# The last 256 hidden features in front of the Strassen units, fewer adding DMAs, sums and loads at new steps

## The chip, the cores and the metric

One core of one Trainium2 chip runs the whole kernel. The metric is the time of one launch in device microseconds; the median of several runs is compared. The engines are TensorE (PE, with its weight loads PEld), VectorE (DVE), ScalarE (ACT), GpSimd (POOL) and SyncE (SP). Each works through its own instructions in order. SP issues most plain DMAs; POOL issues the DMAs that add to their destination and some stores.

## The reference

One layer over 16 meta tokens and 512 tokens of width 1024: a gated feed-forward network, a mixer of retention and selected attention, a second feed-forward network, a norm. The change lies at the mixer's end and in the second network.

```python
D_MODEL, SEQ, D_FF, N_META = 1024, 512, 2816, 16
def rmsnorm(x, g):
    y = x * lax.rsqrt(jnp.mean(x * x, axis=-1, keepdims=True) + EPS)
    return y * g
def swiglu(u, w_gate, w_up, w_down):
    return (jax.nn.silu(u @ w_gate) * (u @ w_up)) @ w_down
h = h + 0.5 * swiglu(rmsnorm(h, ffn1_norm), ffn1_w_gate, ffn1_w_up, ffn1_w_down)
h = h + hybrid_mixer(rmsnorm(h, mix_norm), ...)        # ends with merged @ w_mix_out
h = h + 0.5 * swiglu(rmsnorm(h, ffn2_norm), ffn2_w_gate, ffn2_w_up, ffn2_w_down)
return rmsnorm(h, final_norm)[:, N_META:]
```

## The kernel before

Every float32 product is made of three matmuls in a rounded format: each operand is split into an upper part (ACT copies it, `whi`) and a lower part (the rest, `wlo`), and upper x upper, upper x lower and lower x upper are summed in PSUM. The lower part is made in one of two ways: `in_two` lets DVE subtract the upper part from the source, `in_two_by_pool` lets ACT write the negative upper part and a DMA issued by POOL add the source to it ("adding DMA"; such a step is called far, `is_far`).

The mixer's last product, `merged @ w_mix_out`, is made in eight rounds (`mixed(c)`, PSUM tile `psmo`). Each adds the residual (`hc`), writes the new tokens of 128 features (`new_x`, split into `xh` and `xl`), and takes the squares for the norm.

The second network's gate and up products over 2816 hidden features are made in two kinds of work. 2560 features are five **units** of 512 features: unit u makes gate and up together as a 2x2 block product by Strassen's way with seven products instead of eight (`PRODUCTS`), each in two steps, so 14 steps a unit and 12 matmuls of 128x512 a step. For this, weights are summed (`Unit.sums`: n 0 makes `s1`, 1 makes `s2`, 3 and 4 change `21` and `12` in place) and so are tokens (T1 to T4, made by `token_sums` and split by `split_token_sum`). The PSUM tiles are `psvX`, `psvZ`, `psvY`. The remaining **256 features** (`last_run`, PSUM tile `psl`, weights in `glast`) are four steps of 24 plain matmuls with no sums, behind unit 4.

`run_units` writes the order out by hand: `ahead(i)` says how many steps ahead a step's weights are begun (ACT's upper part), `lower()` puts the lower part in the middle of a step, and `behind(i)` stands at the end of a step: evictions from PSUM, Silu, `finish(i)` of the unit before (scaling by the norm, transposes `turn`, stores `leave` to the DRAM tile `hx`), sums for this or the next unit (`SUMS`, `FIRST_SUMS`), loads for the next (`LOADS`). `norm_column` sums the squares by small matmuls (`psn`). PE, ACT and DVE keep that order (`tc.manual_schedule`); `in_order` and `pool_order` keep a DMA's place on SP or POOL.

Weights lie in a pool of pairs (`pair_of`, 128x1024 elements a tile, most tags with one buffer); a load into a pair waits until the old content has been split and summed. Units 1 and 3 keep the first halves of `12` and `21` in `f2["extra"]`. Even steps' split weights have three buffers (`whi`, `wlo`), odd ones two (`dhi`, `dlo`).

Behind the units comes the down product (`psd`, then the Strassen products X, Y, U, W, V, Z, Q with `half_product`), fed by hidden rows read back from `hx` (`read_hidden`), weights `wd2`, block sums `wx` that were made during the mixer (`block_sums`; `late_sums` makes the last of them in its rounds), and tokens read back from `ht`. `todo` and `behind` hold work that is popped in the middle of its steps.

## Time and profile before

| what | value |
|---|---|
| time, median of 3 runs | 1498.04 us (1497.08 to 1506.18) |
| the profiled execution's own time | 1496.0 us |
| its span, first to last instruction | 1494.2 us |
| mean granted TensorE clock | 0.995 |
| PE busy | 1470.4 us, 98% |
| DVE / ACT / POOL busy | 1146.6 / 803.4 / 272.9 us |
| mixer's last product (`psmo`) | 1102.0 to 1145.5 us |
| units 0 to 4 | 1145.5 to 1356.6 us |
| last 256 features (`psl`) | 1356.6 to 1378.4 us |
| down product | 1378.4 us to the end |

The page lists the busy time of each engine, DMA queues, the chain of work that ended last, and groups of instructions with their mean duration. A line such as `L2685` is a line of the kernel; `psvX<-whi,th` names the tile written and the tiles read. Views of the same trace that were asked for beside it: busy times by stretches of the span, waits (who waited for whom: total, times, longest), instructions in order of time (start, duration, engine, line, operation; in brackets the idle time before and what ended it), and groups of instructions of one engine or tile. The profile is of one execution; matmuls overlap, so their start-to-start distance is what counts.

### The profile page before, as it was taken

The page shows a single profiled execution, that of the slowest core. Times are in us where ns is not written, and L with a number is a line of the kernel's source. Part 1 is how long each engine was busy: PE and PEld are TensorE (multiplying, and loading weights), DVE is VectorE, ACT ScalarE, POOL GpSimd, SP SyncE. Part 2 cuts the span into 40 slices and gives each one's busy share as a digit, 9 for nine tenths or more (in the row PEclk, how much of TensorE's full clock was granted, in tenths as well). Part 3 has the DMA queues.
Part 4 walks back from the last instruction along what each step waited for, and adds up shares of the span by engine and source line. Part 5 has one row for each costly group of instructions (what it writes and reads, how often), then busy time and mean ns, then how long its engine had stood idle before and what let it go on. Part 6 is the DMA issues. An engine that isn't in the chain of part 4 may idle for free.

```text
span 1494.2 us, 23045 instructions
## 1 busy us (share of the span) xinstructions
PE 1470.4 (98%) x8709; PEld 1296.9 (87%) x8709; DVE 1146.6 (77%) x1718; ACT 803.4 (54%) x1200; POOL 272.9 (18%) x397
## 2 busy tenths in 40 slices
PE   9999999999999999999999999999999899999998
PEld 8999999999988888889898888898787688788886
DVE  4999999788886768677868776877568667687778
ACT  5655555566354445553434446776436666563555
POOL 1012222001110121112110121220205134344001
PEclk9999999999999999999999999999999999999999
DMA  5358988786554444679976688666757899899874
GB/s 178 86 180 270 267 265 265 264 294 208 201 174 149 165 148 153 143 211 198 235 200 177 171 227 236 187 188 182 226 196 219 235 222 233 198 224 281 301 257 147
DMA packets 212142, 312.37 MB, mean 209 GB/s; under 512 B 13440, under 2 KB 129816, under 8 KB 211136
## 3 DMA queue, kind: packets, MB, share of 16 engines
q1 hardware_dynamic: 168832, 217.91, 44.9%
q0 software_dynamic: 40672, 88.74, 25.7%
q10 hardware_dynamic: 2528, 4.27, 0.8%
q8 instruction: 68, 1.11, 0.3%
q14 instruction: 42, 0.34, 0.1%
HBM read 220.66 MB, written 63.98 MB: 190 GB/s over the span
## 4 chain that ended last, share of the span: by engine, by line
PE 81%; DMA 7%; DVE 6%; issue 3%; ACT 3%; POOL 1%; SPq 0%; POOLq 0%; ACTq 0%; DVEq 0%
PE psqX L176 7%; PE psrg L176 6%; PE psro L176 5%; PE psvX L1373 4%; PE psqY L176 3%; PE psrk L176 3%; PE psvX L2685 3%; PE psrq L176 3%; PE psga L176 3%; PE psat L176 2%; PE psX L1048 2%; PE psak L176 2%; PE psd L3021 2%; PE psgate L176 2%; PE psvY L1373 2%
## 5 line engine op out<-in xcount | busy, mean ns | idle before, releaser
L314 DVE TENSOR_TENSOR wlo<-raw,whi 128x1024 fp32r<-128x1024 f32 (+2 forms) x181 | 200.6, 1109 | 58.5 <-ACT whi L313 57.9
L313 ACT ACTIVATE whi<-raw 128x1024 fp32r<-128x1024 f32 (+2 forms) x181 | 174.9, 967 | 127.0 <-PE psX L1048 12.2
L176 PE MATMUL psro<-vo,whi 128*128 128x512 f32 x256 | 75.3, 389 | 0.0
L176 PE MATMUL psqX<-th,whi 128*128 128x264 f32 x216 | 61.5, 285 | 1.9 <-DVE g L546 1.9
L176 PE MATMUL psqX<-tl,whi 128*128 128x264 f32 x216 | 61.2, 283 | 0.0
L176 PE MATMUL psqX<-th,wlo 128*128 128x264 f32 x216 | 61.1, 283 | 0.0
L176 PEld LDWEIGHTS psro<-vo,whi 128*128 128x128 f32 x256 | 48.1, 188 | 10.0
L320 POOL DMA_DIRECT2D wlo<-raw x21 | 28.4, 1379 | 151.7 <-ACT wlo L319 55.2
L956 POOL DMA_DIRECT2D hx<-z x72 | 50.1, 810 | 21.5 <-DVE z L2758 16.6
L314 DVE TENSOR_TENSOR wlo<-w,whi 128x1024 fp32r<-128x1024 f32 x35 | 42.6, 1221 | 13.1 <-ACT whi L313 13.1
L176 PE MATMUL psrg<-xh,whi 128*128 128x512 f32 x128 | 50.5, 394 | 0.0
L176 PE MATMUL psrg<-xl,whi 128*128 128x512 f32 x128 | 50.0, 390 | 0.0
L313 ACT ACTIVATE whi<-w 128x1024 fp32r<-128x1024 f32 x35 | 36.9, 1056 | 20.6 <-PE psvX L1373 10.9
L313 ACT ACTIVATE whi<-wsum 128x1024 fp32r<-128x1024 f32 x36 | 38.1, 1058 | 17.9 <-issue 7.3
L176 PE MATMUL psro<-vo,wlo 128*128 128x512 f32 x128 | 46.4, 390 | 0.6 <-DMA wlo<-raw 0.6
L314 DVE TENSOR_TENSOR dlo<-w,dhi 128x1024 fp32r<-128x1024 f32 x23 | 28.0, 1219 | 22.8 <-ACT dhi L313 22.8
L314 DVE TENSOR_TENSOR wlo<-wsum,whi 128x1024 fp32r<-128x1024 f32 x36 | 43.5, 1220 | 0.1
L176 PEld LDWEIGHTS psqX<-th,whi 128*128 128x128 f32 x216 | 40.6, 188 | 2.5 <-DVE g L546 2.3
L176 PE MATMUL psat<-vo,whi 128*128 128x512 f32 x128 | 40.8, 400 | 1.1 <-ACT whi L117 1.1
L176 PEld LDWEIGHTS psqX<-th,wlo 128*128 128x128 f32 x216 | 40.6, 188 | 0.0
L176 PEld LDWEIGHTS psqX<-tl,whi 128*128 128x128 f32 x216 | 40.6, 188 | 0.0
L2311 POOL DMA_DIRECT2D pt<-turned x32 | 20.8, 658 | 104.6 <-DVE turned L2305 98.1
(658 smaller groups left out, 5084.6 us busy)
## 6 DMA issues: line engine op xcount, KB each, us to landing
raw<-in_w_in_dram SPq DMA_DIRECT2D x35, 512.0 KB, 5.1
raw<-in_ffn_w_down_dram SPq DMA_DIRECT2D x34, 512.0 KB, 4.5
raw<-in_w_in_dram SPq DMA_DIRECT2D x17, 1024.0 KB, 6.0
raw<-wx SPq DMA_DIRECT2D x32, 512.0 KB, 4.8
w<-in_w_in_dram SPq DMA_DIRECT2D x24, 512.0 KB, 6.4
raw<-in_ffn_w_up_dram SPq DMA_DIRECT2D x11, 1024.0 KB, 7.9
wlo<-raw POOLq DMA_DIRECT2D x21, 512.0 KB, 6.1
raw<-in_ffn_w_gate_dram SPq DMA_DIRECT2D x10, 1024.0 KB, 6.5
```

Of the source, the lines that this page charges most:

```text
L176: nc.tensor.matmul(o, a[:, k, :], b[:, sl], start=first and k == 0 and i == 0, stop=last and k == nk - 1 and i == 2, skip_group_check=onto)
L313: nc.scalar.activation(hi, src, AF.Copy)
L314: return lambda: nc.vector.tensor_tensor(lo, src, hi.bitcast(F32), ALU.subtract)
L320: return lambda: nc.gpsimd.dma_start(lo, src, accum_op=ALU.add)
L956: tc.keep_in_program_order(nc.gpsimd.dma_start(*args, **how))
L1048: nc.tensor.matmul(pss[c], a[:, k, c * P : (c + 1) * P], m[:, k, :], start=first and k == 0 and i == 0, stop=last and k == 1 and i == 2, s ...
L1373: nc.tensor.matmul(d[bank_][t], a, b[:, k, :], start=not onto and j + k + m == 0, stop=j + k == 3 and m == 2, skip_group_check=onto)
L2311: nc.gpsimd.dma_start(d.rearrange("m b k (a q) -> a k (m b) q", a=4)[a], z[32 * a : 32 * a + 32, :16].rearrange("k b j q -> k b (j q)"))
L2685: nc.tensor.matmul(d[bank_][:, t], a, b[:, k, :], start=not onto and j + k + m == 0, stop=j + k == 3 and m == 2, skip_group_check=onto)
L3021: nc.tensor.matmul(ps, a[:, bs], m[:, j, :], start=first and i == 0, stop=last and i == 2, skip_group_check=onto)
```

## The change

The 256 last features move from behind unit 4 to a place between the mixer's last product and unit 0; their weights are loaded during mixer rounds 2 to 5, and unit 0's first loads and splits move back accordingly. The token sums' splits and `norm_column` stand behind their four steps, `last_scale`, `last_turn` and `last_leave` behind unit 0's steps 0 to 2. The weights' sums leave `behind` for the middle of a step, up to a step and a half earlier. Loads for the next unit stand at most one behind a step, in another order and starting at step 0. Only steps 4, 6, 8 and 12 stay far: four adding DMAs a unit where units 1 to 4 had seven and unit 0 five; some lower parts are made one to four steps behind their upper parts. Units 1 to 4 leave out one transpose and half a store that nobody reads. The moves of the mixer's `late_sums` keep their place on POOL. At the other end, unit 4's steps 10 to 13 and the down product's first loads and splits interleave, unit 4's `finish` runs in the middle of the first four down steps, T4 gets a pool of its own (later also two hidden blocks), the down product's weights lie in a new pool, its last eviction is done in two halves, and two PSUM pools change places.

```diff
-        LOADS = {4: (("11", 0),), 5: (("21", 0),), 6: (("11", 2),), 7: (("22", 0), ("12", 0)), 8: (("21", 2),),
-                 10: (("12", 2),), 11: (("22", 2),)}
-        SUMS = {1: ((1, 2),), 2: ((3, 0),), 4: ((4, 0),), 5: ((3, 2),), 7: ((4, 2),)}
-        FIRST_SUMS = {1: ((1, 2),), 3: ((3, 0),), 5: ((4, 0), (3, 2)), 7: ((4, 2),)}
-        SPLITS = {0: ((2, 1), (4, 1)), 1: ((2, 0),), 2: ((1, 0), (1, 1)), 4: ((3, 0), (3, 1)), 7: ((4, 0),)}
+        LOADS = {0: ("12", 0), 1: ("21", 0), 2: ("11", 0), 4: ("22", 0), 5: ("11", 2), 7: ("21", 2), 9: ("12", 2), 10: ("22", 2)}
+        SUMS = {0: ((0, 2),), 1: ((1, 2), (3, 0)), 2: ((4, 0),), 4: ((4, 2),), 5: ((3, 2),)}
+        NEXT = {10: (0, 0), 11: (1, 0)}
+        UNUSED = [(u, 0, 1) for u in range(1, 5)]
...
         def is_far(self, i):
-            return i % 2 == 0 if self.u else i in (2, 3, 6, 8, 10)
+            return i in (4, 6, 8, 12)
 
         def ahead(self, i):
-            if not self.is_far(i):
-                return 3
-            return 5 if self.u else 4
+
+            first = {0: 2, 1: 2, 2: 3, 4: 4}
+            if not self.u and i in first:
+                return first[i], 0
+            return {0: (5, 4), 2: (5, 1), 10: (5, 2)}.get(i, (5 - i % 2 * 2, 0))
 
         def upper(self, i):
 
             v = self.q[self.PRODUCTS[i // 2][0], i % 2 * 2]
-            where = "raw" if not self.u and i in (2, 3) else "odd" if i % 2 and (self.u or i > 1) else None
-            return parts(v, where, (in_two, in_two_by_pool)[self.is_far(i)])
+            return parts(v, i % 2 == 1, (in_two, in_two_by_pool)[self.is_far(i)])
...
                         lower()
+                        for at in self.SUMS.get(i, ()):
+                            if self.u or at[0] > 1:
+                                self.sums(*at)
+                        if self.next and i in self.NEXT:
+                            self.next.sums(*self.NEXT[i])
...
                 p.finish(i)
-            else:
...
-                if i == 0:
-                    token_sums(KD - 1)
-                for n, at in self.SPLITS.get(i, ()):
-                    split_token_sum(n, at)
-                if i == 4:
-                    norm_column()
-                if i == 6:
-                    self.load("22", 0)
-                    self.load("22", 2)
-            for n, j in (self.SUMS if p else self.FIRST_SUMS).get(i, ()):
-                if p and n == 1:
-                    self.sums(0, j)
-                self.sums(n, j)
-            nxt = self.next
-            if nxt:
-                for n, j in self.LOADS.get(i, ()):
-                    nxt.load(n, j)
-                if i in (11, 12):
-                    nxt.sums(i - 11, 0)
-            else:
-                for g in {4: (0,), 6: (1,), 7: (2, 3)}.get(i, ()):
-                    load_last(g)
+            elif i in (0, 1, 2):
+                (last_scale, last_turn, last_leave)[i]()
+            if self.next and i in self.LOADS:
+                self.next.load(*self.LOADS[i])
...
-                nc.vector.transpose(z[:, u], self.d["H"][:, v % 2 * 2 + v // 2])
+                if (self.u, n, u) not in self.UNUSED:
+                    nc.vector.transpose(z[:, u], self.d["H"][:, v % 2 * 2 + v // 2])
...
-            z = self.d["z", n]
+            z, m = self.d["z", n], 1 + ((self.u, n, 1) not in self.UNUSED)
...
-        t = glast[g] = pair_of(("w110", "w112", "s10", "s12")[g])
+        if g not in glast:
+            glast[g] = pair_of(("w120", "w122")[g - 2])
+        t = glast[g]
         for i, w in enumerate((wg2, wu2)):
...
+            if b == 1:
                 lower()
-        for n in ((0, 3, 4, 5), (6, 7), (8, 9), (10, 12))[g]:
-            units[4].finish(n)
+        behind_last(g)
+
+    def behind_last(g):
+
+        un = units[0]
+        for n, j in {0: (("11", 2),), 1: (("12", 0), ("12", 2)), 2: (("22", 0), ("22", 2))}.get(g, ()):
+            un.load(n, j)
+        if g == 0:
+            token_sums(KD - 1)
+        elif g == 1:
+            f2["ss"] = room2(1, "ss")[:, :, : 2 * P]
+            for t in range(2):
+                nc.scalar.activation(f2["ss"][:, t].rearrange("p (b a y) -> p a b y", b=2, a=4),
+                                     ssum3[:, t * 2 * P : (t + 1) * 2 * P].rearrange("p (a b y) -> p a b y", b=2, a=4), AF.Copy)
+        elif g == 2:
+            norm_column()
+        else:
+            last_silu()
+        for n, at in {0: ((2, 1), (4, 1), (2, 0)), 1: ((4, 0), (1, 0), (1, 1), (3, 0)), 2: ((3, 1),)}.get(g, ()):
+            split_token_sum(n, at)
+        if g > 1:
+            un.sums(1, g * 2 - 4)
 
     def last_silu():
...
-                  for un in units for i in range(14)]
-        steps_ += [(lambda g=g: parts(glast[g]), lambda *a, g=g: last_run(g, *a), 2 + (g < 3)) for g in range(4)]
-        ws, begin = {}, {}
-        for i, (upper, _, ahead_) in enumerate(steps_):
-            if i > 3:
-                begin.setdefault(i - ahead_, []).append(i)
...
+        for i, (_, _, (ahead_, later_)) in enumerate(steps_):
+            begin.setdefault(i - ahead_, []).append(i)
+            end.setdefault(i - ahead_ + later_, []).append(i)
+        for j in range(2):
+            ws[j] = steps_[j][0]()
...
         for i, (_, run, _) in enumerate(steps_):
-            now = begin.get(i, ())
-            for j in now:
+            for j in begin.get(i, ()):
                 ws[j] = steps_[j][0]()
-            run(ws.pop(i)[:2], lambda: [ws[j][2]() for j in now])
+            run(ws[i][:2], lambda: [ws[j][2]() for j in end.get(i, ())])
             yield
...
         late_sums = block_sums(range(EARLY_SUMS, 8), lambda: [block_room(t) for t in ("R", "ssum2", "caus", "score3")],
-                               nc.gpsimd.dma_start)
+                               pool_order)
         cols = mo_cols
-        EARLY = {2: (("11", 0), ("11", 2)), 3: (("s1", 0),), 4: (("12", 0), ("s1", 2)), 5: (("12", 2), ("21", 0)), 6: (("21", 2),)}
+        EARLY = {2: (0,), 3: (1,), 4: (2, ("s1", 0)), 5: (3, ("s1", 2)), 6: (("21", 0),), 7: (("11", 0), ("21", 2))}
         one, two = slice(0, 2 * P), slice(2 * P, S)
         firsts, hcs = [pair_of(t) for t in ("s20", "s22")], []
-        for j in (0, 2):
-            units[0].q["11", j] = pair_of(f"w11{j}")
+        for g in range(2):
...
-                if n == "s1":
-                    units[0].added_load(j)
+            for at in EARLY.get(c, ()):
+                if at in range(4):
+                    load_last(at)
+                elif at[0] == "s1":
+                    units[0].added_load(at[1])
                 else:
-                    units[0].load(n, j, in_order)
-            if c >= 5:
+                    units[0].load(*at, in_order)
+            if c >= 6:
                 next(unit_pipe)
                 next(unit_pipe)
...
             squares_go(c)
             if c in (1, 3, 5):
                 token_sums(c)
-            if c == 6:
...
-        f2["odd"] = tts.enter_context(pool("f2d", 1, side="right"))
-        f2["z"], f2["extra"] = (wpool.tile([P, 2048], F32, tag="raw", name=name, bufs=2).rearrange("p (a k c) -> p a k c", a=2, k=2)
-                                for name in ("z", "extra"))
...
-            hid[f] = tuple(f2["hid"].tile([P, S], F32R, tag=f"h{c}{f}", name=f"h{c}") for c in "hl")
+            if f < F0:
+                hid[f] = tuple(f2["hid"].tile([P, S], F32R, tag=f"h{c}{f}", name=f"h{c}") for c in "hl")
+            else:
+                both = ttp4.tile([P, 2, S], F32R, tag=f"t{'hl'[f - F1]}4", name="hh")
+                hid[f] = both[:, 0], both[:, 1]
             return in_two(hid[f, "raw"], *hid[f])
 
...
-                        d["raw"] = wpool.tile([P, 2048], F32, tag="raw", name="raw", bufs=2).rearrange("p (k c) -> p k c", k=4)
+                        d["raw"] = fin["p"].tile([P, 2048], F32, tag="raw", name="raw", bufs=2).rearrange("p (k c) -> p k c", k=4)
...
+                        def add(bs):
+                            for b in bs:
+                                add_sums(b, slice(c * S, (c + 1) * S), d["ps"][b])
+
+                        if c:
+                            add((0, 1))
+                            behind.append(lambda add=add: add((2, 3)))
+                        else:
+                            add(range(4))
 
                 steps.append((pre, lambda at=at: d[at], run))
...
         with tc.manual_schedule(engines=BUSY):
-            for _ in range(14 * 5):
...
             f2["hid"] = hids2.enter_context(pool("hid2", 1, side="right"))
-            next(unit_pipe)
             for f in range(3):
                 read_hidden(f)
-            for i in range(3):
-                read_tokens(i)
+            next(unit_pipe)
+            units_on.close()
+            hpool = later.enter_context(pool("hpool", 1))
+            hTok.extend(hpool.tile([P, D], F32, tag=f"hTok{b}", name=f"hTok{b}") for b in range(4))
+            fp = fin["p"] = later.enter_context(pool("f2", 1))
+            homes.append(fp)
+            next(pipe)
             lows = [split_hidden(f) for f in range(2)]
             next(unit_pipe)
             for low in lows:
                 low()
             read_hidden(3)
-            lows = [split_hidden(f) for f in (2, 3)]
-            next(unit_pipe)
-            for low in lows:
-                low()
             next(pipe)
             next(pipe)
             next(unit_pipe)
             next(pipe)
-            next(pipe)
...
-            hTok.extend(hpool.tile([P, D], F32, tag=f"hTok{b}", name=f"hTok{b}") for b in range(4))
-            fp = fin["p"] = later.enter_context(pool("f2", 1))
-            homes.append(fp)
+            lows = [split_hidden(f) for f in (2, 3)]
+            for i in range(3):
+                read_tokens(i)
+            for f in (F1, F1 + 1):
+                read_hidden(f)
+            next(unit_pipe)
+            for low in lows:
+                low()
+
+            def steps_of_last(*steps):
+                for i in steps:
+                    units[4].finish(i)
 
             def begin():
 
-                last_silu()
+                steps_of_last(0, 3, 4)
                 for i in range(3):
                     take_tokens(i)
                     read_tokens(3 + i)
-                last_scale()
-                last_turn()
 
             def go_on():
 
-                last_leave()
+                steps_of_last(5, 6, 7)
                 for i in range(3, 6):
                     take_tokens(i)
                     if i < 5:
                         read_tokens(3 + i)
 
-            todo += [begin, go_on, lambda: [f(i) for f, i in ((read_hidden, F1), (read_hidden, F1 + 1), (take_tokens, 6), (take_tokens, 7))],
+            todo += [begin, go_on, lambda: (steps_of_last(8, 9, 10), take_tokens(6), take_tokens(7)), lambda: steps_of_last(12),
                      lambda: None, lambda: split_hidden(F1)(), lambda: split_hidden(F1 + 1)()]
             for _ in range(n_plain):
                 next(pipe)
             mm_done()
-            ends = later.enter_context(pool("f2px", 2, PSUM))
+            ends = later.enter_context(pool("f2pe", 6, PSUM))
+            pb["pool"] = later.enter_context(pool("f2px", 2, PSUM))
+            next(pipe)
             pb["pool"] = ends
-            next(pipe)
-            pb["pool"] = later.enter_context(pool("f2pe", 6, PSUM))
             next(pipe)
             gfb = fin["gfb"] = fp.tile([P, D], F32, tag="gfb", name="gfb")
```

More of the change, by code (lines that the diff above doesn't have):

```diff
@@ L2846, in split_token_sum @@
         part = t[:, :, 2 * P :] if n in (2, 3) else t[:, :, : 2 * P]
-        split(part, *(p[:, n - 1, 2 * i : 2 * i + 2, :] for p in f2["tt"]))
+        split(part, *(p[:, 2 * i : 2 * i + 2, :] for p in f2["tt"][n - 1]))
     def token_sums(c):
@@ L2871, in run_units @@
     def run_units():
[L2873 to L2882 removed]
+        steps_ = [(lambda g=g: parts(glast[g]), lambda *a, g=g: last_run(g, *a), (2, 0)) for g in range(4)]
+        steps_ += [(lambda un=un, i=i: un.upper(i), lambda *a, un=un, i=i: un.run(i, *a), un.ahead(i))
+                   for un in units for i in range(14)]
+        ws, begin, end = {}, {}, {}
+        for i, (_, _, (ahead_, later_)) in enumerate(steps_):
[3 more added lines that the diff above has]
+            ws[j] = steps_[j][0]()
             yield
[L2884 to L2885 removed]
+            ws[j][2]()
             yield
         for i, (_, run, _) in enumerate(steps_):
[L2888 to L2889 removed]
+            for j in begin.get(i, ()):
                 ws[j] = steps_[j][0]()
[L2891 removed]
+            run(ws[i][:2], lambda: [ws[j][2]() for j in end.get(i, ())])
             yield
@@ L2957, in mixed @@
                 token_sums(c)
-            if c == 6:
-                units[0].sums(1, 0)
         with tc.manual_schedule(engines=BUSY):
@@ L3059 @@
         todo = []
-        def keep(b, c):
-            pass
         fin = {}
@@ L3110, in leave @@
             nc.scalar.dma_start(out[rows, 512:], hTok[b][:, 512:])
-        streams, ahead, behind, homes = {}, [4], [], [wpool]
+        streams, ahead, behind, homes, spare = {}, [4], [], [wpool], ["dhi", "dlo"]
         SLOT = {0: 0, 1: 1, 2: 2, 3: 3, 4: 4, 5: 7, 6: 5, 7: 6}
@@ L3201, in sums_of @@
             return lambda j: wx[i, :, 2 * j : 2 * j + 2, :]
-        steps = down(0, 4, 4, keep)[0]
+        steps = down(0, 4, 4)[0]
         n_plain = len(steps)
         steps += product("X", rows(0, C1), 0, added((0, C1)))
-        steps += down(F1, 2, 2, keep)[0]
+        steps += down(F1, 2, 2)[0]
         steps += product("Y", sums_of(0), 4, added((1, C2)))
@@ L3216 @@
         with tc.manual_schedule(engines=BUSY):
-            for _ in range(14 * 5):
+            for _ in range(4 + 14 * 4 + 10):
                 next(unit_pipe)
```

53 lines of the change are left out of this document (19 added, 34 removed).

## The prediction

> **What bounds the kernel now.** First the page's head, for the engines' shares.
>
> ```profile
> span 1494.2 us, 23045 instructions
> PE 1470.4 (98%) x8709; PEld 1296.9 (87%) x8709; DVE 1146.6 (77%) x1718; ACT 803.4 (54%) x1200; POOL 272.9 (18%) x397
> ```
>
> PE is busy for 98% of the span. No matmul is added or taken away by the change, so all it can win are pauses of PE, and all it can lose are new ones. Next comes the view by stretches, over the part that the diff touches, cut where products begin: unit 0, units 1 to 4 (168 matmuls each), the last 256 features (96 matmuls, `psl`), the first down steps, the rest, the tail. Its columns are the stretch, its length, the busy time of PE, PEld, DVE, ACT and POOL (with instructions), PE's granted clock, the DMA engines' share and GB/s.
>
> ```profile
> 1145.50:1196.10 50.60, 43.82 (x178) 34.35 (x177) 35.17 (x39) 35.93 (x47) 13.40 (x13) 0.93 0.80 208
> 1196.10:1234.90 38.80, 38.80 (x170) 31.51 (x169) 26.29 (x27) 26.14 (x29) 11.35 (x15) 1.00 0.92 224
> 1234.90:1273.70 38.80, 38.80 (x169) 31.56 (x168) 30.31 (x33) 25.46 (x28) 15.91 (x22) 1.00 0.92 234
> 1273.70:1316.70 43.00, 39.68 (x169) 31.33 (x168) 30.31 (x34) 25.88 (x28) 16.64 (x24) 1.00 0.87 205
> 1316.70:1356.60 39.90, 39.32 (x169) 31.39 (x168) 30.78 (x33) 23.43 (x26) 15.90 (x23) 1.00 0.88 216
> 1356.60:1378.40 21.80, 21.80 (x97) 18.02 (x97) 16.09 (x22) 5.74 (x8) 10.27 (x16) 1.00 0.94 300
> 1378.40:1400.40 22.00, 22.00 (x97) 18.05 (x97) 12.67 (x20) 11.64 (x19) 2.57 (x4) 1.00 0.80 281
> 1400.40:1484.40 84.00, 84.00 (x371) 69.46 (x370) 70.95 (x97) 49.08 (x70) 4.48 (x2) 1.00 0.71 243
> ```
>
> A unit without pauses takes 38.8 us (units 1 and 2). Unit 0 takes 50.6, unit 3 43.0, unit 4 39.9: 11.8 + 4.2 + 1.1 = 17.1 us above that. From 1356.6 to 1484.4 PE never pauses, and the 9.8 us behind that are the output's, which the diff leaves as they are. The waits of PE in these stretches and the instructions that make up the first unit's norm say what the 17.1 us are:
>
> ```profile
> PE psvY L2685 <- DMA wlo<-w: 2.7, 1, 2.7
> PE psvX L2685 <- ACT th L117: 2.0, 1, 2.0
> PE psvX L2685 <- ACT part L2696: 1.8, 1, 1.8
> PE psvX L2685 <- DMA wlo<-w: 1.4, 2, 1.0
> PE psvX L2685 <- ACT dhi L313: 1.0, 1, 1.0
> PE psvY L2685 <- ACT part L2696: 0.9, 1, 0.9
> PE psvX L2685 <- DVE dlo L314: 0.5, 1, 0.5
> ```
>
> ```profile
> 1163.27 0.95 PE L2866 MATMUL psn<-ones,ss 128*128 128x1 f32 x8
> 1187.13 0.63 PE L2685 MATMUL psvY<-dlo,xh 128*128 128x512 f32 x1
> 1187.56 0.63 PE L2685 MATMUL psvY<-dhi,xh 128*128 128x512 f32 x1
> ```
>
> The pauses themselves are 10.3 us. Behind the longest ones matmuls start 0.43 us apart (the last two rows), where 38.8 / 168 = 0.231 is usual: unit 0's clock of 0.93 is that, some 3 us. 0.95 us of unit 0 are the eight `psn` matmuls, which stay. **What can be won is 17.1 - 0.95 = 16.2 us**, 1.1% of the time; 10.9 of it lie in unit 0.
>
> **The change, part by part.**
>
> *The last 256 features first.* Unit 0 pauses because its weights' sums, the token sums T1 to T4 and their splits all have to be made beside its own matmuls: `th` (a token sum) is late by 2.0, adding DMAs by 2.7 and 1.0. The last features need plain tokens and unsummed weights. Their 21.8 us (sixth stretch) now stand between the mixer and unit 0, with DVE and ACT free for those sums. Is that enough? DVE is behind when the mixer ends:
>
> ```profile
> 1149.33 0.68 DVE L2943 TENSOR_TENSOR hc<-psmo,hc 128x512 f32<-128x512 f32 x1
> ...
> 1152.38 1.75 DVE L2859 TENSOR_TENSOR s<-s,w 128x512 f32<-128x512 f32 x1
> ```
>
> ```profile
> 1230.67 1.22 DVE L2641 TENSOR_TENSOR s<-w,w 128x1024 f32<-128x1024 f32 x1
> 1231.80 1.22 DVE L314 TENSOR_TENSOR dlo<-w,dhi 128x1024 fp32r<-128x1024 f32 x1
> ```
>
> Token sums can begin at about 1152.4. A 128x1024 instruction of DVE keeps it for 1.13 us (from 1230.67 to 1231.80), one of 128x512 for 0.69. From 1152.4 DVE has three token sums (3.1 us), eight token splits (5.5), the splits of the last two groups of the last features (2.3), those of unit 0's first three steps (3.4) and two sums for `s2` (2.3): 16.6 us, done near 1169.0. Unit 0's first step starts at 1145.5 + 21.8 + 0.9 (`psn`) = 1168.2; the split it needs stands some 5 us ahead of the end of that list, and T2 is needed four steps later. I cost it at nothing. If the list ran 3 us late, the cover would still hold; at 6 us PE would wait. In the mixer's last rounds the splits of unit 0's first four steps make way for two of the last features: on DVE two for two, and one sum (1.13 us) leaves with them, so DVE is no later than now. Step 4 of unit 0 takes its operand by an adding DMA which ACT can only prepare behind `last_silu`:
>
> ```profile
> 1176.76 1.28 ACT L2738 ACT_TABLE_LOAD   x1
> L2816 ACT ACTIVATE sg<-psl,r x4: 457/470/483, 1383.2 to 1384.2; 128x256 f32<-128x256 f32 x4
> L2583 ACT ACTIVATE wlo<-w 128x1024 fp32r<-128x1024 f32 x4 | 4.2, 1043 | 0.0
> DMA to landing us min/median/max: 4.4/6.9/12.6
> ```
>
> From the end of `psl` (1168.2): table 1.3, four silus 1.6, a split 1.0, the two copies 2.0, so the DMA starts at 1174.1 and lands after 4.4 to 12.6 us, at 1181.0 by the median. Its half of step 4 begins at 1168.2 + 4 x 2.77 + 8 x 0.231 = 1181.1. PE waits between 0 and 5.6 us; I take 1.0. The Trainium skill ("DMA: Bandwidth & Descriptors", Anatomy of one DMA) fits a GpSimd transfer as 2.0 us plus bytes at 436 GB/s, an estimate of 3.2 us for 512 KB. By that fit this wait would be zero and the sum 1.0 us lower; the 4.4 us minimum here is above it, so the rows decide.
>
> *Four adding DMAs a unit instead of seven.* DMA in the five units:
>
> ```profile
> q0 software_dynamic: 7759, 25.70, 57.8%
> wlo<-w POOLq DMA_DIRECT2D x16, 512.0 KB, 9.1
> w<-in_ffn_w_up_dram SPq DMA_DIRECT2D x16, 512.0 KB, 9.2
> ```
>
> The software queue takes 57.8% of 211.5 us with 33 adding DMAs of 512 KB among its 25.70 MB (33 x 0.524 = 17.3): by bytes 82 us, an estimate of 2.5 us of all 16 engines for each. Three fewer take 7.5 of 38.8 us: the share of 0.92 falls to about 0.73, and a load lands sooner than 9.2. The price: each of the three becomes one DVE subtraction (+1.13) and saves one ACT copy (-1.0).
>
> ```profile
> L2758 DVE STREAM_TRANSPOSE z<-H 128x512 f32<-128x512 f32 x8 | 5.2, 689 | 1.9 <-DMA hx<-z 1.9
> L314 DVE TENSOR_TENSOR dlo<-w,dhi 128x1024 fp32r<-128x1024 f32 x5 | 6.1, 1217 | 4.6 <-ACT dhi L313 4.6
> ```
>
> DVE in a unit (unit 2, third stretch): 30.3 + 3 x 1.13 - 0.7 (one transpose left out) = 33.0 of 38.8, 85%. The eighth stretch ran DVE at 70.95 of 84.0, 84%, and PE never paused: so a share like this can be covered. Of unit 2's 8.5 idle us 4.6 are waits for ACT's upper part, and ACT gets 3 us lighter. Bounds for units 1 to 4 together: 0 to 4 x (33.0 + 8.5 - 38.8) = 10.8 us, if none of DVE's idle time can shrink. I take 1.0, near the row of the eighth stretch.
>
> *Sums mid step, one load a step.* Unit 3's 4.2 us:
>
> ```profile
> 1269.51 3.39 SPq L2622 DMA_DIRECT2D w<-in_ffn_w_up_dram  x2
> 1285.15 1.23 DVE L2641 TENSOR_TENSOR s<-w,w 128x1024 f32<-128x1024 f32 x1 [5.78 <-DMA w<-in_ffn_w_up_dram]
> 1288.84 0.50 PE L2685 MATMUL psvX<-dhi,th 128*128 128x512 f32 x1 [1.04 <-ACT dhi L313]
> ```
>
> The two up-loads went out from 1269.5 on and DVE stood in front of the sum of both until 1285.2, up to 15.7 us later; the matmuls of step 5 (1288.8) hang on it. The last load (`22`, second half) moves from step 11 to 10 and the one ahead of it from 8 to 7, 2.8 us each. The sum now stands in step 0 instead of behind step 1; behind it on DVE wait the previous unit's scaling, two more sums and the split of step 5, and PE waits for that split. With the loads earlier and DMA lighter I cost this at nothing beyond the 1.0 above. Pinning the `wx` moves costs nothing either: POOL is busy 16 of 39 us in a unit, and PE waits for none of them.
>
> *Handover to the down product.* Before, `psl`'s 21.8 us covered unit 4's `finish`, the reading of hidden rows and the first `wd2` loads. Now these begin at unit 4's step 9 to 13, 11 us ahead of the first down step, and `finish` runs inside down steps 0 to 3.
>
> ```profile
> raw<-in_ffn_w_down_dram SPq DMA_DIRECT2D x34, 512.0 KB, 4.5
> 1374.74 1.06 ACT L313 ACTIVATE whi<-raw 128x1024 fp32r<-128x1024 f32 x1 [1.47 <-DMA raw<-in_ffn_w_down_dram]
> ```
>
> Unit 4 loads nothing more (before, eight `glast` loads), so its queue is free. Three hidden rows and four loads of 512 KB go out between 10.9 us (end of step 9) and some 7 us (the last split, step 10) ahead of the down step; the first weights land 4.5 us later, then 1.06 on ACT and 1.13 on DVE: 10.9 - 6.7 = 4.2 us early at best, 7 - 6.7 = 0.3 at worst by the median, and with a landing of 9.2 us (the up-loads' row) 4.4 us late. I take 1.0. `finish` brings DVE its eight turns (5.2 us by the row above) and about as much again into a stretch that had 12.7 of 22.0, while the last features' scale and turn (3 us) leave it: some 20 of 21.8, tight, but its evictions have banks to spare. I keep it inside the same 4.4.
>
> **The sum**, against the profiled execution's own 1496.0 us (its span of 1494.2 and 1.8 around it): 1496.0 - 16.2 + 1.0 + 1.0 + 1.0 = 1482.8 us. The three runs of before have their median at 1498.04, 2.0 above it, their lowest 1.1 above; I add 1.5 and predict **1484 us**.
>
> **The rivals.**
> *DVE becomes the bound.* For it: 85% in program order, with 4.6 us of waits for ACT inside. Against: the eighth stretch. Its price is the 10.8 us above in place of 1.0: 1484 + 9.8 = 1494.
> *The first unit still pauses*, because DVE is behind at the mixer's end by 3.8 us (1149.3 against 1145.5) and the chain from token sums to splits is serial with ACT. For it: pauses there were ACT's `th` and `part`. Against: 21.8 us of cover for 16.6 of work. If the 16.6 stretch to 26, as when every instruction takes 1.75 for 0.69 (the token sum at 1152.4) for a while, 8 of the 10.9 us stay: 1492.
> *A late load stops DVE in every unit: slower than before.* The sum in step 0 holds the whole DVE order, and 33.0 of 38.8 leave it 5.8 us to catch up. If the second `22` load lands in units 1 to 4 as late as in unit 3 (DVE stood 5.8 us), and DVE's spare time is used by its waits for ACT, all of it reaches PE: 4 x 5.8 = 23.2, so 1484 - 1.0 + 23.2 = 1506. It decides from a landing about 9 us into the unit (step 5 at 13.9 less two sums, a copy and a split, 4.6). Against: the load goes out 2.8 us earlier, into a queue at 0.73.
> *The change does not do what it says* would be a first unit that starts without its sums ready, which is the second rival.
>
> **How the numbers follow.** Chances: forecast 0.62 (1480 to 1488), DVE bound 0.18, first unit 0.09, late load 0.11. A measurement of this kernel tells about 1% from no change, 15 us: under 1483 is faster, over 1513 slower. The forecast's lower four tenths or so lie under 1483: with all three terms near zero it is 1481. That makes faster 0.28; slower only the late load beyond its own price, 0.04; the same 0.68. The range takes in the first two rivals and leaves out the slow one: 1479.5 to 1497.
>
> The Trainium skill has one more rule that bears on what is left ("TensorE: Matmul & The Clock Gate", Part 1: The HAM clock gate): the clock is halved after an idle window of about 3.4 us. Here pauses of 2.0 and 2.7 us were enough (the 0.43 us starts), so the trace does not agree; by the rule the pauses I left in would cost only their length, by the rows one of over 2 us costs about 1.5 more.
>
> **What would show it.** In the profile of the changed kernel: `psl` right behind `psmo` with no pause; unit 0 at 40 us and not 50.6; units 1 to 4 at 38.8 to 39.5; DVE at some 33 us a unit; the DMA share near 0.73 and `wlo` adds landing under 9.1; no `th` and no `w` of the up-loads among PE's waits; the first `psd` directly behind unit 4. Wrong would make it: DVE waits for loads at the `s` sums, PE waits for `dlo` or `wlo` of DVE in each unit, or a pause ahead of `psd`.

## The result

The changed kernel takes **1476.61 us** (median of six runs, 1475.91 to 1477.45) where the kernel before, beside it, takes 1497.61 (1495.60 to 1506.18): a ratio of 0.985, 95% interval 0.9827 to 0.9873. The prediction was 1484 with a range from 1479.5; the kernel is 7.4 us faster than that and 3 us below the range. The profiled execution took 1477.45 us, its span is 1475.7.

The engines' shares, from the head of the page after:

```profile
PE 1463.6 (99%) x8709; PEld 1294.2 (88%) x8709; DVE 1157.4 (78%) x1727; ACT 792.9 (54%) x1187; POOL 257.9 (17%) x384
```

The view by stretches (columns as in the prediction: stretch, length, PE, PEld, DVE, ACT, POOL, clock, DMA share, GB/s). The rows are the last 256 features with the eight `psn` matmuls, and units 0 to 4:

```profile
1139.85:1164.59 24.74, 23.02 (x105) 18.84 (x104) 20.30 (x25) 16.39 (x26) 6.64 (x7) 1.00 0.67 211
1164.59:1203.40 38.81, 38.81 (x170) 31.54 (x169) 25.96 (x29) 26.05 (x29) 6.84 (x9) 1.00 0.71 190
1203.40:1242.25 38.85, 38.85 (x170) 31.54 (x169) 29.59 (x30) 23.61 (x25) 8.68 (x13) 1.00 0.72 189
1242.25:1281.10 38.85, 38.85 (x170) 31.54 (x169) 33.46 (x35) 23.61 (x25) 13.33 (x21) 1.00 0.79 210
1281.10:1319.95 38.85, 38.85 (x170) 31.54 (x169) 33.74 (x36) 23.61 (x25) 13.70 (x21) 1.00 0.68 169
1319.95:1358.80 38.85, 38.85 (x170) 31.54 (x169) 30.91 (x34) 21.88 (x25) 13.41 (x20) 1.00 0.68 172
```

All five units take 38.8 us and PE never pauses in them. The list of PE's waits from 1040 to 1475 us has one row:

```profile
PE psl L2786 <- DVE hc L2942: 1.7, 1, 1.7
```

**Where the 18.55 us between the two profiled executions lie.** From the mixer's end to the first down step: 1378.40 - 1145.50 = 232.9 before, 1358.80 - 1139.85 = 218.95 after, so 14.0. In front of the mixer's last product 5.6 us, of which the prediction knew nothing: that product starts at 1101.97 before and at 1096.33 after. Behind the first down step 1.1 us are lost (115.8 to 116.9).

The 5.6 us. Two stretches from 1055 us to the start of that product, before and then after; PE's two waits there before (after has none); and POOL's and DVE's instructions around them, before and then after (start, duration, engine, line, operation; in brackets the idle time before it and what ended it):

```profile
1055.00:1101.97 46.97, 44.23 (x191) 35.96 (x190) 27.15 (x36) 15.70 (x22) 5.55 (x6) 0.96 0.71 240
1055.00:1096.30 41.30, 41.30 (x187) 34.36 (x186) 26.83 (x35) 14.82 (x22) 5.60 (x7) 1.00 0.79 269
```

```profile
PE psat L176 <- DVE wlo L118: 1.7, 1, 1.7
PE psat L176 <- ACT whi L117: 1.1, 1, 1.1
```

```profile
1059.33 1.23 POOL L1588 DMA_DIRECT2D wq<-in_ffn_w_down_dram  x2 [10.45 <-DVE ptl L314]
...
1070.28 0.69 DVE L2551 SCALAR_TENSOR_TENSOR sa<-sa,psat 128x512 f32<-128x512 f32 x1 [7.15 <-DMA sa<-gd]
```

```profile
1068.73 1.29 POOL L1643 TENSOR_TENSOR accr<-accr,gate 128x512 f32<-128x512 f32 x1 [2.64 <-DMA gate<-gd]
1069.97 2.18 POOL L956 DMA_DIRECT2D wq<-in_ffn_w_down_dram  x4
...
1065.49 0.69 DVE L2551 SCALAR_TENSOR_TENSOR sa<-sa,psat 128x512 f32<-128x512 f32 x1 [3.12 <-DMA sa<-gd]
```

`late_sums` does not only move `wx`: it first loads its operands, the down weights `wq`. Before, those loads had no fixed place, and some stood on POOL from 1059.3 us on, in front of the reads of `gate` and `sa` that the mixer was waiting for (ACT issues them from 1061.9 on). DVE waited 7.15 us for `sa`, and PE behind it. Pinned, the first four loads come at 1070, behind the additions to `accr`, and DVE waits 3.12. (0.8 of the 5.6 us were there before 1046 already: the `pt` stores start at 1045.05 instead of 1045.82.)

### The profile page after: what moved, and what is told of

Same layout as the page of the kernel before. It is cut to its first block, busy times and chain, and to the rows that moved or that the text cites. A ratio compares the mean times of both kernels' runs of the same rounds, so it can differ in the third digit from the quotient of the medians.

```text
span 1475.7 us, 23006 instructions
## 1 busy us (share of the span) xinstructions
PE 1463.6 (99%) x8709; PEld 1294.2 (88%) x8709; DVE 1157.4 (78%) x1727; ACT 792.9 (54%) x1187; POOL 257.9 (17%) x384
## 4 chain that ended last, share of the span: by engine, by line
PE 92%; DMA 2%; DVE 2%; ACT 1%; issue 1%; SPq 0%; POOL 0%; POOLq 0%; ACTq 0%; DVEq 0%
PE psvX L2682 8%; PE psrg L176 6%; PE psqX L176 6%; PE psro L176 6%; PE psvX L1373 4%; PE psvY L2682 4%; PE psga L176 3%; PE psrk L176 3%; PE psrq L176 3%; PE psat L176 3%; PE psak L176 3%; PE psqY L176 3%; PE psaq L176 3%; PE psX L1048 2%; PE psd L176 2%; PE psd L3024 2%
## 5 line engine op out<-in xcount | busy, mean ns | idle before, releaser
L314 DVE TENSOR_TENSOR wlo<-w,whi 128x1024 fp32r<-128x1024 f32 x45 | 54.9, 1227 | 14.1 <-ACT whi L313 14.1
L313 ACT ACTIVATE whi<-w 128x1024 fp32r<-128x1024 f32 x45 | 47.4, 1056 | 27.3 <-PE psvX L1373 10.9
L956 POOL DMA_DIRECT2D hx<-z x72 | 45.7, 645 | 51.3 <-DVE z L2736 51.0
L176 PE MATMUL psrg<-xh,whi 128*128 128x512 f32 x128 | 50.4, 394 | 0.0
```

Source lines behind the costliest of these rows:

```text
L176: nc.tensor.matmul(o, a[:, k, :], b[:, sl], start=first and k == 0 and i == 0, stop=last and k == nk - 1 and i == 2, skip_group_check=onto)
L313: nc.scalar.activation(hi, src, AF.Copy)
L314: return lambda: nc.vector.tensor_tensor(lo, src, hi.bitcast(F32), ALU.subtract)
L956: tc.keep_in_program_order(nc.gpsimd.dma_start(*args, **how))
```

## The experiments

The kernels ran in three groups, each on one chip with its own runs of the kernel before, so differences are taken within a group where that is possible. The medians of the kernel before are 1495.51, 1493.75 and 1495.14 us in groups 1, 2 and 3. Group 2 has no run of the changed kernel: its runs are held against each other, and by their ratios.

| kernel | median us | ratio to before, interval |
|---|---|---|
| changed kernel (group 1) | 1475.33 | 0.987 (0.9854 to 0.9887) |
| changed, moves not pinned | 1482.02 | 0.9913 (0.9896 to 0.993) |
| before, moves pinned | 1489.61 | 0.9966 (0.9952 to 0.9981) |
| order of the last features, handover and pinning alone | 1487.21 | 0.994 (0.9921 to 0.9958) |
| changed, seven adds (group 2) | 1475.87 | 0.9873 (0.9858 to 0.9888) |
| changed, old loads | 1476.30 | 0.9875 (0.986 to 0.9891) |
| changed, old sums | 1481.27 | 0.9911 (0.9895 to 0.9927) |
| changed, bank order | 1475.57 | 0.9872 (0.9856 to 0.9887) |
| changed, seven adds and old sums (group 3) | 1485.18 | 0.9936 (0.9913 to 0.996) |
| changed, seven adds and old loads | 1475.91 | 0.9879 (0.9851 to 0.9906) |
| changed, bank order and wider tiles | 1477.42 | 0.9884 (0.986 to 0.9908) |
| changed kernel (group 3) | 1477.16 | 0.9884 (0.986 to 0.9908) |

### Does pinning carry the 5.6 us?

The changed kernel again, as the measure of its group:

> The changed kernel itself, as the measure for the others of this group. Both theories: 1476.6 us, within 1.5 us of the first measurement, with no wait of the attention output (psat) for its weights and one pause of 1.7 us at psl.

Its median was 1475.33. The changed kernel without the pinning:

```diff
-                               pool_order)
+                               nc.gpsimd.dma_start)
```

> The changed kernel, only the moves of the late block sums are again left to the planner (plain POOL DMAs instead of pinned ones). Theory P (the gain beyond the forecast's bound came from the pinning: unpinned, three wq loads stand on POOL ahead of the two accr additions and the sa and gate loads land some 4 us later): 1481 us, 4 to 5 above the changed kernel, psat waits of about 1.1 and 1.7 us for its split weights back, the sa wait of DVE near 7 us instead of 3. Rival C (those 5 us are chance between executions or come from other addresses): 1476.6 us, no psat waits.

It takes 6.7 us more than the changed kernel beside it (4.2 between the two profiled spans), and PE's waits of before are back, next to the one at `psl`, which stays:

```profile
PE psat L176 <- ACT whi L117: 1.5, 1, 1.5
PE psat L176 <- DVE wlo L118: 1.3, 1, 1.3
```

The kernel before with the same one line pinned (the diff the other way round):

> The kernel before, only the moves of the late block sums are pinned on POOL. Theory P: 1492.5 to 1493.5 us, 4 to 5 below the kernel before, without the psat waits; units as before (unit 0 near 50 us). Rival C: 1497.5 us as before.

It takes 5.9 us less than before. The `psat` waits are gone, and the stretch up to the mixer's last product has no pause left:

```profile
1055.00:1100.19 45.19, 45.19 (x204) 37.55 (x203) 29.19 (x40) 16.74 (x24) 5.62 (x7) 1.00 0.82 278
```

One line is worth about 6 us in either kernel, more than the 4 to 5 expected. That this line is the cause is shown by both. That it works through the early loads fits the traces: DVE's first wait for `sa` is 7.15 us before and 7.18 in the unpinned kernel, where loads of `wq` stand in front, and 3.12, 3.80 and 3.48 in the changed kernel, its second run and the pinned kernel before, where none does. That the loads do it by taking DMA time from `gate` and `sa` is a reading of these rows; the loads were not moved by themselves.

### What is the new order of the features worth alone?

The changed kernel with seven adds in units 1 to 4, the old places of loads and the old places of sums (the three diffs below together); the order of the last features, the handover to the down product that goes with it, and the pinning stay.

> The changed kernel with the order, the pinning and the handover kept, but seven adding DMAs a unit in units 1 to 4, the loads behind the same steps as in the kernel before, and the sums at the steps' ends at their old places. Theory O (the order covers unit 0's 10.9 us; the pauses of units 3 and 4, 5.3 us, came from late loads in a DMA system at a share of 0.92 and return): 1480 to 1482 us, unit 0 at 38.8 us, DMA share near 0.9 in the units, a DVE wait for the up-loads again. Rival S (the order alone did it, the other three edits are worth nothing): 1476.6 us with no pause in units 1 to 4. Rival T (mid-step sums and early loads are what keeps DVE in time even in unit 0): above 1485 us.

1487.21, only 2.4 below the pinned kernel before, and the two intervals overlap. Its waits of PE from 1040 us on:

```profile
PE psd L3028 <- DVE wlo L314: 2.0, 1, 2.0
PE psl L2790 <- DVE hc L2946: 1.7, 1, 1.7
PE psd L3028 <- ACT hh L313: 1.4, 1, 1.4
PE psvX L2685 <- ACT dhi L313: 1.2, 1, 1.2
PE psvZ L2685 <- DMA wlo<-extra: 1.2, 1, 1.2
PE psvX L2685 <- DVE dlo L314: 0.5, 1, 0.5
```

The first unit's pauses are gone, as the prediction had it: by the starts of its matmuls unit 0 takes 38.8 us, and 50.4 in the pinned kernel before. But PE now waits 3.4 us at the first down step (`psd`) and 1.7 at `psl`, and unit 3, which paused before the change too, takes 44.4 us instead of 42.0 (2.9 of waits). Together the waits are 8.0, where the pinned kernel before had 10.7 in its units; slower starts behind some of them come on top. The gain was given back later, and the three undone edits together hold 1487.21 - 1475.33 = 11.9 us. The time is the one of rival T, but its reason, a DVE that is late in unit 0, did not occur; theory O lacked the handover.

### Which of the three?

Each undone by itself. Seven adds:

```diff
-            return i in (4, 6, 8, 12)
+            return i % 2 == 0 if self.u else i in (4, 6, 8, 12)
...
+            if self.u:
+                return 5 - i % 2 * 2, 0
```

> The changed kernel with one part undone: units 1 to 4 take seven adding DMAs of 512 KB each again instead of four (the splits of those steps are begun where four-add steps' neighbours are begun); loads, sums, the new order of the last features and the pinned moves stay. The order alone (all three undone) gave 1487.2 on the chip where the changed kernel gave 1475.3, and its 12 us lie in unit 3 (1285 to 1302: an adding DMA 1.2, a split 1.2 and 0.5, slowed matmuls) and ahead of the first down step (1363 to 1370: hidden rows' split 1.4, weights' split 2.0, slowed matmuls). Theory A (the adding DMAs' traffic makes loads late, there 15 us to landing): most of it comes back, ratio to before 0.991 to 0.996, some 1483 to 1489, with PE waiting for an add in unit 3 and the first down step late. Theory L (two loads in one step): nothing, 0.985 to 0.988. Theory M (only together do the three fill the queue): 0.985 to 0.989 here and in the next two runs alike.

Nothing is lost: 1475.87, and the only wait of PE is the one at `psl`. DVE has this wait in unit 3, which PE doesn't feel:

```profile
DVE s L2637 <- DMA w<-in_ffn_w_up_dram: 4.9, 1, 4.9
```

So theory A fell. The loads:

```diff
-        LOADS = {0: ("12", 0), 1: ("21", 0), 2: ("11", 0), 4: ("22", 0), 5: ("11", 2), 7: ("21", 2), 9: ("12", 2), 10: ("22", 2)}
+        LOADS = {4: (("11", 0),), 5: (("21", 0),), 6: (("11", 2),), 7: (("22", 0), ("12", 0)), 8: (("21", 2),),
+                 10: (("12", 2),), 11: (("22", 2),)}
...
```

> The changed kernel with one part undone: a unit's eight weight loads are issued behind steps 4, 5, 6, 7 (two), 8, 10 and 11 again, instead of one behind each of steps 0, 1, 2, 4, 5, 7, 9 and 10. Sums mid step and four adds stay. The sum of the last load now stands in step 0 but the load goes out a step later, so a late landing stops DVE at once. Theory L (loads' places): ratio to before 0.989 to 0.995, some 1480 to 1488, with DVE waiting for w of the up loads in unit 3 for over 5 us. Theory A (adds): the queue is light, a load lands in under 9 us, nothing is lost: 0.985 to 0.988. Theory M: 0.985 to 0.989.

Nothing either: 1476.30, no new wait. Theory L fell too. The sums:

```diff
-        SUMS = {0: ((0, 2),), 1: ((1, 2), (3, 0)), 2: ((4, 0),), 4: ((4, 2),), 5: ((3, 2),)}
-        NEXT = {10: (0, 0), 11: (1, 0)}
+        SUMS = {1: ((0, 2), (1, 2)), 2: ((3, 0),), 4: ((4, 0),), 5: ((3, 2),), 7: ((4, 2),)}
+        NEXT = {11: (0, 0), 12: (1, 0)}
...
                     if n == 0 and t == 0:
                         lower()
-                        for at in self.SUMS.get(i, ()):
-                            if self.u or at[0] > 1:
-                                self.sums(*at)
...
+            for at in self.SUMS.get(i, ()):
+                if self.u or at[0] > 1:
+                    self.sums(*at)
             if self.next and i in self.LOADS:
```

> The changed kernel with one part undone: the weights' sums stand at steps' ends and at their old places again (the last one behind step 7 instead of in step 4, the last load's first sum behind step 1 instead of in step 0). Four adds and one load a step stay. Theory S (the sums' places): splits come later, PE waits for dlo or dhi in each unit, 4 x 1 to 2 us: 0.988 to 0.993, some 1479 to 1486. Theories A and L: nothing, 0.985 to 0.988. Theory M: 0.985 to 0.989.

1481.27, 5.4 above the run with seven adds: theory S held, and theory M, that only the three together lose anything, did not. A unit now takes 40.1 us, and PE waits 1.0 in each of units 1 to 4. The row of waits, a stretch of a unit's length, and DVE's order around the first of them in this kernel and in the changed one:

```profile
PE psvX L2682 <- DVE wlo L314: 3.9, 4, 1.0
```

```profile
1209.92:1250.02 40.10, 39.13 (x169) 31.46 (x168) 29.68 (x30) 23.50 (x25) 8.71 (x13) 1.00 0.69 184
```

```profile
1201.16 1.22 DVE L314 TENSOR_TENSOR wlo<-extra,whi 128x1024 fp32r<-128x1024 f32 x1
1202.29 1.22 DVE L2640 TENSOR_TENSOR s<-s,w 128x1024 f32<-128x1024 f32 x1
1203.43 1.22 DVE L314 TENSOR_TENSOR wlo<-w,whi 128x1024 fp32r<-128x1024 f32 x1
```

```profile
1200.31 1.22 DVE L314 TENSOR_TENSOR wlo<-extra,whi 128x1024 fp32r<-128x1024 f32 x1
1201.45 1.22 DVE L314 TENSOR_TENSOR wlo<-w,whi 128x1024 fp32r<-128x1024 f32 x1
```

At its old place a sum stands between two splits for the next unit, the one of its step 2 and, behind that, the one of its step 0. The split of step 0 is late by just that sum: 1.13 us of DVE, and 40.10 - 38.85 = 1.25 us a unit with the slower starts behind it. Four times that is 5.0 of the 5.4. DVE is no busier (29.68 against 29.59 in unit 1): what changed is the order, not the load. The sums' steps and their place inside a step were undone together, so which of the two is needed is open.

### Why does the order alone lose 11.9?

With four adds the old sums cost 5.4; with seven those two splits are adding DMAs again and can't wait for that sum, so the 11.9 must be made in another way. Two pairs, first seven adds with the old sums (the first and the third diff together):

> The changed kernel with two parts undone: seven adding DMAs a unit and the sums at steps' ends and old places; one load a step stays. Seven adds alone gave 1475.9 with the one pause of the changed kernel, old sums alone 1481.3 with a split on DVE late by 1.0 in each unit (four times). Theory of pairs (what the order alone loses at the handover, 5.5 us, is adds with sums): the sums of unit 4's last weights come late, so the last adding DMA starts some 10 us later, the first down weights wait for its landing because they go into the room that it leaves, and PE pauses 4 to 6 us ahead of the first psd; no pause in unit 3; and the four waits of 1.0 are gone, since those splits are adding DMAs again: ratio to before 0.990 to 0.993, some 1480 to 1482. Rival (both losses of the order alone come from adds with loads): no pause, 0.986 to 0.988.

1485.18, 8.0 above the changed kernel beside it (1477.16). The waits of 1.0 are gone; these came, and the handover shows how. First its waits; then, in the same kernel, the loads of the first down weights on SP, ACT's wait for them and the first `psd`; then those three in the changed kernel:

```profile
PE psd L3026 <- DVE wlo L314: 2.0, 1, 2.0
...
PE psvX L2684 <- ACT part L2695: 1.5, 1, 1.5
PE psd L3026 <- ACT hh L313: 0.7, 1, 0.7
PE psvX L2684 <- DVE dlo L314: 0.5, 1, 0.5
PE psvX L2684 <- ACT dhi L313: 0.3, 1, 0.3
```

```profile
1354.56 2.57 SPq L952 DMA_DIRECT2D raw<-in_ffn_w_down_dram  x4
1359.57 1.06 ACT L313 ACTIVATE whi<-raw 128x1024 fp32r<-128x1024 f32 x1 [8.71 <-DMA raw<-in_ffn_w_down_dram]
1361.20 0.49 PE L3026 MATMUL psd<-whi,hh 128*128 128x512 f32 x1 [0.72 <-ACT hh L313]
```

```profile
1348.48 3.92 SPq L952 DMA_DIRECT2D raw<-in_ffn_w_down_dram  x4
1353.87 1.06 ACT L313 ACTIVATE whi<-raw 128x1024 fp32r<-128x1024 f32 x1 [5.17 <-DMA raw<-in_ffn_w_down_dram]
1358.78 0.40 PE L3024 MATMUL psd<-whi,hh 128*128 128x512 f32 x1
```

The first down weights go into the room that the units leave, so they wait for the units' last adding DMA (in the list of waits SP stands 7.4 us for `wlo<-w` here, 4.6 in the changed kernel). With sums late that DMA is late, and they go out 6.6 us ahead of `psd` instead of 10.3. The theory of pairs held for the handover. Its "no pause in unit 3" was wrong: 2.3 us of waits are there too, with loads at the new places, and unit 3 takes 42.3 us instead of 38.85. So the time is also above the 1480 to 1482 expected. The other pair is seven adds with the old loads (the first two diffs):

> The changed kernel with two parts undone: seven adding DMAs a unit and the loads at their old places; sums mid step at the new places stay. Old loads alone gave 1476.3, seven adds alone 1475.9, both with the one pause of the changed kernel. Theory of pairs (what the order alone loses in unit 3, 6.1 us, is adds with loads): both up loads for unit 3 go out within 0.5 us of each other into a queue with three adds, land 15 us later, DVE stands at the sum of them, and PE pauses 4 to 6 us in unit 3 and nowhere else: 0.989 to 0.993, some 1479 to 1482. Rival (it takes the old sums too, or it is the sums with the loads): no pause in unit 3, 0.986 to 0.988.

1475.91 and no wait but `psl`'s. Here the rival held: loads cost nothing with or without seven adds, as long as the sums stand where the change puts them. So the sums' places are the part that decides: undone alone 5.4, with seven adds 8.0, with the loads too 11.9 (in another group). What the loads add to the other two (about 3.9, across groups) was not run on one chip.

### Can the pause that is left go?

`psl`'s second PSUM tile lies in the bank of the last mixer product, which DVE reads late. From the changed kernel, DVE's instructions, then PE's:

```profile
1142.26 1.53 DVE L314 TENSOR_TENSOR wlo<-w,whi 128x1024 fp32r<-128x1024 f32 x1 [0.78 <-ACT whi L313]
1143.72 0.68 DVE L2942 TENSOR_TENSOR hc<-psmo,hc 128x512 f32<-128x512 f32 x1
...
1142.35 0.39 PE L2786 MATMUL psl<-wlo,xh 128*128 128x512 f32 x1
1144.45 0.50 PE L2786 MATMUL psl<-whi,xh 128*128 128x512 f32 x1 [1.72 <-DVE hc L2942]
```

The edit takes the two tiles in another order:

```diff
-        for b in range(4):
+        order = {0: ((0, 0), (0, 1)), 1: ((1, 0), (1, 1), (0, 2), (0, 3), (1, 2), (1, 3))}.get(g, [(g, b) for b in range(4)])
+        for n, (h, b) in enumerate(order):
...
```

> The changed kernel with one edit beside it: the last features' first two groups visit their four banks in the order g0 b0 b1, then g1 b0 b1, g0 b2 b3, g1 b2 b3, so that the second PSUM tile, whose bank the last mixer product still holds until DVE has read it, is first written 5.4 us after the stretch begins instead of 2.7 us (and the fourth group's split is begun one step ahead instead of two). The one pause left from 1040 us on in the changed kernel is there, 1.7 us of waiting plus slower starts, 2.0 in all. Theory B (the bank): it goes, 1.5 to 2.2 us less than the changed kernel, ratio 0.983 to 0.986 and no wait of PE in the last 430 us but the output's. Rival (DVE is behind by more than 2.7 us, or the group taken later brings a wait for its split): same time or a new pause, 0.986 to 0.989.

The wait for `hc` goes and a shorter one comes, for the second group's split, which the new order needs 2.7 us sooner:

```profile
PE psl L2788 <- DVE wlo L314: 0.7, 1, 0.7
```

The median, 1475.57, can't be told from its neighbours' 1475.87 and 1476.30. With wider tiles for the odd steps' parts beside it (`P, 1024 + WPAD`, the data 32 bytes further in):

> The changed kernel with two edits beside it, a candidate for a faster one: the last features' bank order of the run before (its one pause was 1.0 us instead of 2.0, its median 1475.6 beside 1475.9 of a kernel with the pause), and the tiles of upper and lower parts in the odd steps and of the last products' token sums made as wide as the other parts' tiles, their data 32 bytes further in. Theory W (where the tiles lie sets the pitch of matmuls): the products behind the first down steps go from 229 to 227 ns a matmul, 10.98 to 10.88 us per 48, some 0.9 us over the eight, and the units perhaps from 231 to 229. In all 1 to 2 us less than the changed kernel, 1473.5 to 1475. Rival (the pitch has nothing to do with the tiles' place): 229 ns as before and 0.5 to 1 us less than the changed kernel, which can't be told from no change.

1477.42 beside 1477.16 for the changed kernel:

> The changed kernel itself, on the chip of the three kernels beside it, so that these stand against it and not only against the kernel before: 0.984 to 0.989 of before, 1474 to 1477, one pause of 2.0 us from 1040 us on, and 229 ns a matmul in the last products.

No version faster than the changed kernel was found. Durations of `psX` matmuls (in ns, least, median, greatest), one row each of before, of the changed kernel and of this one:

```profile
L3162 PE MATMUL psX<-whi,xp x96: 388/389/390, 1400.4 to 1465.6; 128*128 128x512 f32 x96
```

```profile
L3169 PE MATMUL psX<-whi,xp x96: 392/393/394, 1380.8 to 1446.5; 128*128 128x512 f32 x96
```

```profile
L3173 PE MATMUL psX<-whi,xp x93: 388/394/397, 1379.9 to 1445.5; 128*128 128x512 f32 x93
```

From start to start, in lists of PE's instructions, these are 227, 229 and 233 ns; with the bank order alone it is 229, as in the changed kernel. So the edit to the tiles does set it, but my direction was wrong for the down products: the padding made six of them slower by 6 x 48 x 4.4 ns = 1.3 us, about what the bank order gave. In the units the direction was right, if small: a unit takes 38.77 us instead of 38.85.

Not run by themselves are the transpose and the half store that are left out, the new pools and the last eviction in two halves.

## Why the prediction was wrong

**The step that failed: "Pinning the `wx` moves costs nothing either".** It looked at POOL in a unit (busy 16 of 39 us), but `late_sums` runs in the mixer's rounds, and what it issues are loads too. The pinning is worth 5.9 to 6.7 us by the runs; without it the changed kernel takes 1482.02 us, inside the range. The bound "what can be won is 16.2 us" was drawn from 1145.5 us on and left it out, although PE's 2.8 us of waits and the clock of 0.96 in front of the mixer's last product stand in the same profile.

**The 16.2 us were right, the path to them was not as simple.** In the part that the bound covered, 14.0 us came, and 2.0 were lost at `psl` (the gap in its row of starts, 1142.35 to 1144.45, less a usual 0.23, and slower starts): 16.0 without that pause. The 10.9 of them that the prediction saw in unit 0 did come from the order of the features. But the order with its handover, without the other edits, shortened the kernel by 2.4 only, because PE then paused at `psl` and at the first down step, and longer in unit 3. It takes the sums' new places to keep the last two away.

**The three terms of 1.0 were all 0.** The first unit's add for step 4 was costed from 0 to 5.6 us; unit 0 took 38.81 and PE waited for no add. DVE in units 1 to 4 was forecast at 33.0 us and was busy for 29.6 to 33.7; with 5.1 us idle in the fullest unit it never stopped PE, as the eighth stretch of before had suggested. DVE as the bound fell with that. For the handover the bounds on when the weights go out, 10.9 to some 7 us ahead of the down step, were fair, and both ends occur: in the changed kernel it is 10.3, with seven adds and late sums 6.6, and PE pauses.

**"`psl` right behind `psmo` with no pause" was wrong**: 2.0 us for a PSUM bank. The prediction had the row that told of it, `hc` 3.8 us behind the end of `psmo`, and used it only for what DVE has to do.

**DMA came out as said.** Of all DMA in the five units, the software queue and a row of landing times (median us, last column):

```profile
q0 software_dynamic: 5567, 17.57, 40.3%
...
w<-in_ffn_w_up_dram SPq DMA_DIRECT2D x13, 512.0 KB, 4.6
```

The queue fell from 57.8% to 40.3%, an up-load lands after 4.6 us instead of 9.2, an add after 7.0 instead of 9.1, and the DMA share is 0.68 to 0.79 (0.73 forecast). But it paid nothing: with seven adds again the time is the same. There DVE waits 4.9 us in unit 3 for an up-load, goes on 7.3 us into the unit, and PE does not feel it. With the old sums beside the seven adds the same load comes later too: DVE goes on 11.0 us into the unit, after a wait of 5.8, and PE pauses. The late load as a rival did not occur in the changed kernel, though its place was right.

**The sum**, on the profiled execution: 1482.8 - 3.0 (the three terms) - 5.6 (in front of the mixer's last product) + 2.0 (`psl`) + 1.1 (behind the first down step) = 1477.3, measured 1477.45. Apart from the 5.6 the errors cancel (-3.0 + 2.0 + 1.1), which is luck. Of the 1.1 the longer pitch of six products explains 6 x 48 x 2.2 ns = 0.6. The other 2 us between 1484 and 1476.6 are the 1.5 that I added for the median and the 0.8 by which the changed kernel's median lies below its profiled execution, less 0.3 of rounding. In these runs the changed kernel's times are also closer together: 1.5 us from end to end where before's are 10.6 apart.

**The clock.** I wrote that a pause of over 2 us costs about 1.5 more. That is no rule. Before, PE waits 2.0 us for `th` and the matmuls behind it start 0.43 us apart; in the pinned kernel before it waits 2.1 us at the same place and they do not. PE's granted clock is 0.62 from 1158.50 to 1163.00 us in the first and 1.00 from 1153.40 to 1158.00 in the second. In the kernel with seven adds and old sums two shorter pauses (0.72 and 1.97 us of waiting, one matmul between) were followed by matmuls 0.43 us apart for 3 us. The Trainium skill ("TensorE: Matmul & The Clock Gate", Part 1: The HAM clock gate) says that the window of about 3.4 us runs freely. That would let the same pause count or not by where it falls, which agrees with these rows, while "an idle window" taken as a pause of 3.4 us does not; no run here shows the window itself.

## What to carry to other kernels

Bound what an edit can win over the whole span that its instructions can be scheduled in, not over the part that the diff's name points to: a DMA without a fixed place may stand in front of a stranger's critical read. On an engine that is 85% busy in a hand-written order, the places of its instructions can decide before its load does; moving a unit's sums by up to a step and a half was worth more here than a third less traffic on the software queue. When an early stall is removed, run it without the accompanying edits: a stall may come back later, here in unit 3, where a load comes late, and at the handover.

## What was not expected of the hardware

The start-to-start time of the same 128x512 matmul was 227, 229 and 233 ns in three kernels. The step from 229 to 233 came with an edit that changes only where `xp`, the operand that PEld loads, and the odd steps' weights lie; the step from 227 to 229 came with many edits, and that place is its cause too is not shown. Which property of the place does it is open.
